# A two-layer encoder on one core: the low part of every second weight group of the first FFN by a negation and an accumulating DMA

## The chip, the cores and the metric

One core of a Trainium2 chip runs the whole kernel. The metric is the device time of one execution in microseconds (us). The kernel before takes 2468.03 us, the median of two runs.

## What is computed

A trunk of two layers over 256 tokens of width 2048, in float32. Layer 0 has differential attention beside a gated MLP over chunks, layer 1 a gated linear recurrence in both directions. After each mixer stands a SwiGLU feed-forward block (FFN) with 5632 hidden features, and the change lies in the first of the two:

```
def swiglu(h, w_gate, w_up, w_down):
    return (jax.nn.silu(h @ w_gate) * (h @ w_up)) @ w_down

    hn = rms_norm(h, ffn_norm[l])
    h = h + swiglu(hn, ffn_w_gate[l], ffn_w_up[l], ffn_w_down[l])
```

## The kernel before

All weight products go through one function, `stream` (L101). It multiplies the 256 tokens (two blocks of 128, each with its own PSUM bank) with 512 columns of a weight matrix, over a list of weight groups. A group is 512 rows by 512 columns, 1 MB, laid out in HBM as one contiguous piece and in SBUF as 128 partitions x 4 x 512.

The products keep float32 precision by splitting. Activations x and weights w are each the sum of a high part, rounded to the type float32r, and a low part, the rest. Per group:

- SP loads the group into `raw` (L114), a tile of a pool with three buffers.
- ACT copies it to `whi` (L121), which rounds it. Three buffers.
- DVE subtracts `whi` from `raw` into `wlo` (L122). Two buffers.
- PE does 24 matmuls, for each of 4 row blocks and 2 token blocks three: x high by w high (L136), x high by w low (L137), x low by w high (L138).

The copy and the subtraction are issued with a priority that places them up to 400 instructions ahead on their engines (`AHEAD`), so ACT and DVE prepare groups ahead of PE as far as the buffers go. A copy has to wait until PE has done with the group three before it, a load until `raw` of the group three before it has been read by ACT and DVE.

`ffn` (L232) runs in two passes over the hidden blocks, 6 and then 5 of them, 512 features each. For each block it calls `stream` for gate and for up, with 4 groups each. After a pass it calls `stream` four times for down, with 6 and then 5 groups each. In between stand a sigmoid on ACT (L249), products on DVE (L250, L255), and transposes of the result by PE with copies by ACT (L173) and subtractions by DVE (L174). The first FFN has 22 x 4 + 4 x 6 + 4 x 5 = 132 groups. Its hidden blocks are held in a pool `hp` (L234). GpSimd (POOL) has nothing but one small power (L153) to do in that stage.

Of the kernel before, what the change touches and what calls it, by code (L numbers as in the profile page):

```python
# [11 lines left out]
F32 = mybir.dt.float32  # L12
# [8 lines left out]
P = 128  # L21
# [3 lines left out]
KG = 4  # L25
# [12 lines left out]
def _ap(base, offset, dims):  # L38
    """View of a tile: its partitions, then [stride, count] dims from `offset`."""
    return bass.AP(base.tensor, base.offset + offset, [list(base.ap[0])] + [list(d) for d in dims])  # L40
# [6 lines left out]
class Lazy:  # L47
    """Operands that are emitted one by one, in order, when they are asked for."""

# [11 lines left out]
def trunk(ctx: ExitStack, tc: tile.TileContext, ins, out):  # L61
# [22 lines left out]

    # ---- work that is emitted in pieces between the groups of a stream
    pieces = []
# [12 lines left out]

    # ---- shared pieces  # L100
    def stream(w, nb, kgs, xs, name, after=None, fine=False, by_block=False):  # L101
        """Two PSUM banks (token blocks) of x @ w[:, nb], over the K groups `kgs`, xs.get(i) the operand of kgs[i]."""
        ps = [ps_mm.tile([P, NB], F32, tag="mm", name=f"{name}_ps{b}") for b in range(2)]
        last = len(kgs) - 1
        held = []
        xs.get(0)
        for i, kg in enumerate(kgs):
            raw = wpool.tile([P, KG, NB], F32, tag="raw", name=f"{name}_raw{i}")
            whi = wpool.tile([P, KG, NB], F32R, tag="whi", name=f"{name}_whi{i}")
            wlo = wpool.tile([P, KG, NB], F32R, tag="wlo", name=f"{name}_wlo{i}", bufs=WLO_BUFS)  # L110
            step = 1 if fine and i == 0 else KG
            for k in range(0, KG, step):
                d = slice(k, k + step)
                nc.sync.dma_start(raw[:, d], w[nb, kg, :, d])  # L114
                with ExitStack() as order:
                    if not fine:
                        order.enter_context(tc.high_priority(offset=AHEAD))
                    elif i == 0 and k > 0:
                        order.enter_context(tc.issue_after(marks["act"]))
                        order.enter_context(tc.issue_after(marks["dve"]))  # L120
                    nc.scalar.copy(whi[:, d], raw[:, d])  # L121
                    nc.vector.tensor_tensor(wlo[:, d], raw[:, d], whi[:, d].bitcast(F32), op=ALU.subtract)  # L122
            if i < last:
                xs.get(i + 1)
            held.append((i, xs.get(i), whi, wlo))
            if by_block and i == last - 1:
                continue
            order = [(g, k, b) for g in held for k in range(KG) for b in range(2)]
            if by_block and i == last:
                order = [(g, k, b) for b in range(2) for g in held for k in range(KG)]  # L130
            held = []
            for n, ((j, (xh, xl), hi, lo), k, b) in enumerate(order):
                sl = slice(b * P, (b + 1) * P)
                first = j == 0 and k == 0
                end = j == last and k == KG - 1
                nc.tensor.matmul(ps[b], xh[:, k, sl], hi[:, k, :], start=first, stop=False)  # L136
                nc.tensor.matmul(ps[b], xh[:, k, sl], lo[:, k, :], start=False, stop=False)  # L137
                nc.tensor.matmul(ps[b], xl[:, k, sl], hi[:, k, :], start=False, stop=end)  # L138
                if n == KG - 1:
                    tick()  # L140
            if after is not None:
                after(i)
            tick()
        return ps
# [16 lines left out]
    def to_T(src, pool, tag, name, gains=None):  # L161
        """Token-major [P, 2, 512] to feature-major high and low parts [P, 4, 256]."""
        xh = pool.tile([P, KG, S], F32R, tag=tag, name=f"{name}_hi")
        xl = pool.tile([P, KG, S], F32R, tag=tag, name=f"{name}_lo")
        for half in range(2):
            tp = ps_tr.tile([P, 2, S], F32, tag="tr", name=f"{name}_tp{half}")
            for c in range(2):
                f0 = (half * 2 + c) * P
                for b in range(2):
                    nc.tensor.transpose(tp[:, c, b * P:(b + 1) * P], src[:, b, f0:f0 + P], ident)  # L170
            if gains is None:
                d = slice(half * 2, half * 2 + 2)
                nc.scalar.copy(xh[:, d, :], tp)  # L173
                nc.vector.tensor_tensor(xl[:, d, :], tp, xh[:, d, :].bitcast(F32), op=ALU.subtract)  # L174
            else:
                for c in range(2):
                    k = half * 2 + c
                    g = gains[k]
                    marks["act"] = nc.scalar.activation(xh[:, k, :], tp[:, c, :], AF.Copy, scale=g).ins
                    marks["dve"] = nc.vector.scalar_tensor_tensor(  # L180
                        out=xl[:, k, :], in0=tp[:, c, :], scalar=g, in1=xh[:, k, :].bitcast(F32),
                        op0=ALU.mult, op1=ALU.subtract).ins
        return xh, xl
# [4 lines left out]
    def mean_square(tiles, name):  # L188
        """Calls that add a tile's part each; the last one leaves the rsqrt in the list."""
        ss = small.tile([P, 2, 4], F32, tag="ss", name=f"{name}_ss")  # L190
# [41 lines left out]
    def ffn(l, xs, rstd, following):  # L232
        """SwiGLU in two passes over the hidden blocks; `following` takes the last pass's hooks."""
        with tc.tile_pool(name=f"hT{l}", bufs=12, reuse_waits="tile") as hp:  # L234
            for blocks in (range(0, 6), range(6, 11)):
# [6 lines left out]
                for j in blocks:  # L242
                    n = f"f{l}_{j}"
                    pg = stream(ins["w_gate"][l], j, ALLK, xs, f"{n}g", after=late)
                    gs = []
                    for b in range(2):
# [4 lines left out]
                        gs.append(sg)  # L251
                    pu = stream(ins["w_up"][l], j, ALLK, xs, f"{n}u")
                    hh = tmp.tile([P, 2, NB], F32, tag="hh", name=f"{n}_hh", bufs=2)
# [5 lines left out]
                for nb in range(4):  # L259
                    pd = stream(ins["w_down"][l], nb, list(blocks), hts, f"f{l}d{blocks[0]}_{nb}",  # L260
                                after=(lambda i, nb=nb: following(nb, i)) if last else None,
                                by_block=last and l == 1 and nb == 3)
                    if last and l == 1:
# [3 lines left out]

    # ---- layer 0 mixer
    xs, rstd, squares = norm(SM_MIX, "e", load=True)
# [29 lines left out]
    def gelu(nb, name, **kw):  # L299
        """gelu(y) as 0.5 y (1 + tanh(c (y + 0.044715 y^3))), with yh = y / 2."""  # L300
        ps, t = proj(nb, name, **kw)
# [11 lines left out]
    def attention(half, qt, kt, vt, o):  # L313
        """Four heads; one head's scores run while another's softmax is at work."""
        qks, es, aTs = {}, {}, {}
# [166 lines left out]

    # ---- layer 1 mixer
    odd = ExitStack()
# [13 lines left out]
    def scan_pair(pair, qt, ft, vt, o):  # L498
        """Two heads. A[t, s] = sum_k q_t k_s prod(decays between), built for ever larger blocks: in each
        block of 2m positions the queries of one half and the keys of the other meet at the boundary."""  # L500
        n = f"s{pair}"
# [16 lines left out]
        for d in range(2):  # L518
            tp = transposed(ft[1 - d], f"tf{d}")
            for i in range(2):  # L520
                hd = pair * 2 + i
                nc.vector.tensor_scalar(F[:, d, i, :], tp[:, i, :], omlb[:, 1 - d, hd:hd + 1], lb[:, 1 - d, hd:hd + 1],
                                        op0=ALU.mult, op1=ALU.add)
            # F holds the backward decays first, K the forward keys first
            nc.vector.tensor_scalar(K[:, 1 - d], F[:, d], -1.0, 1.0, op0=ALU.mult, op1=ALU.add)
# [15 lines left out]
        diag = _ap(A, 0, [[512, 2], [384, 2], [1, P]])  # L541
        # each position with itself, then level by level the pairs that meet there
        sc = scores("ld", lambda i, b: kd[:, i, b * P:(b + 1) * P], lambda i, b: qs[:, i, b * P:(b + 1) * P])
# [48 lines left out]
    for hg in range(4):  # L592
# [4 lines left out]
        if hg == 0:  # L597
# [3 lines left out]
            nc.gpsimd.tensor_copy(masks, mraw[:, 0:7])  # L601
            # softmax over the two layers, then the second one's cumulative sum less the first
            lraw = sm[:, SM_LB:SM_LB + 64].rearrange("p (d l h) -> p d l h", d=2, l=2)
# [57 lines left out]

    # ---- last FFN and the final norm
    fp = ctx.enter_context(tc.tile_pool(name="fin", bufs=1, reuse_waits="tile"))
# [36 lines left out]
def _blocks(w):  # L700
    """[K, N] as [N / 512, K / 512, 128, 4, 512], so that one load is one contiguous piece."""
    k, n = w.shape
# [3 lines left out]
def _cols(a):  # L706
    """[..., n * 128] as [128, ... * n]: features on partitions."""
    a = np.asarray(a)
# [15 lines left out]
def _masks():  # L724
    """[s, which, t]: for each m the pairs in one block of 2m but not in one half of it."""
    i = np.arange(P)
# [48 lines left out]
```

## Time and profile before

| | before |
|---|---|
| median of two runs | 2468.03 us (2466.86 to 2469.21) |
| span of the profiled execution | 2467.0 us |
| busy: PE, DVE, ACT, POOL | 99%, 56%, 42%, 3% |
| share of the 16 DMA engines' time | 52% |
| HBM read | 441.61 MB |

The profile gives no time of the profiled execution apart from its span; that span lies within the range of the two runs and 1.0 us below their median. Names in the rows leave out numbers, so `f_2g` stands for the gate stream of hidden block 2 in both FFNs, while `f0d` is the down stream of the first FFN alone. An "idle before" with an arrow names what ended the wait.

### The profile page before, as it was taken

The numbers are of one execution on the slowest core, as the hardware profiler recorded it, in microseconds if no ns is written. First come the engines' busy times: TensorE is split into PE (matmuls) and PEld (weight loads), VectorE is DVE, ScalarE is ACT, GpSimd is POOL, SyncE is SP. The second block draws the span as 40 slices with busy tenths as digits, with TensorE's granted clock in tenths as the row PEclk, the third lists the DMA queues.
The fourth block names the chain that finished last, engine by engine and source line by source line (L and its number), as shares of the span: only waits on it lengthen the run. The fifth ranks groups of instructions, "written<-read, shape, count | busy, mean of one in ns | idle before, by whom it ended". The sixth has DMA issues, their size and how long they took to land.

```text
span 2467.0 us, 27323 instructions
## 1 busy us (share of the span) xinstructions
PE 2446.4 (99%) x11392; PEld 2033.3 (82%) x11392; DVE 1373.6 (56%) x1192; ACT 1030.8 (42%) x952; POOL 72.3 (3%) x71
## 2 busy tenths in 40 slices
PE   8999999999999999999999999999999999999998
PEld 7887888888888888888888888888888888888887
DVE  5668655454444554444768585855545454444544
ACT  5445444333333343444444444454443433334433
POOL 0003000000000000000000000000000000000001
PEclk9999999999999999999999999999999999999999
DMA  7444455555555555555444444455555555555553
GB/s 270 168 163 162 157 186 188 190 194 188 186 190 192 188 188 188 188 191 191 154 154 154 154 140 156 148 178 192 188 188 192 188 188 188 193 193 188 193 188 136
DMA packets 63132, 445.48 MB, mean 181 GB/s; under 512 B 6944, under 2 KB 7200, under 8 KB 9760
## 3 DMA queue, kind: packets, MB, share of 16 engines
q1 hardware_dynamic: 62576, 442.13, 52.1%
q8 instruction: 89, 1.46, 0.2%
q10 hardware_dynamic: 432, 1.60, 0.2%
q14 instruction: 35, 0.29, 0.0%
HBM read 441.61 MB, written 2.10 MB: 180 GB/s over the span
## 4 chain that ended last, share of the span: by engine, by line
PE 97%; DVE 2%; POOL 1%; issue 0%; DMA 0%; ACT 0%; POOLq 0%; ACTq 0%; DVEq 0%
PE f0d_ps L137 3%; PE f0d_ps L138 3%; PE f0d_ps L136 3%; PE f1d_ps L137 3%; PE f1d_ps L136 3%; PE f1d_ps L138 3%; PE c_f_ps L136 2%; PE c_f_ps L138 2%; PE c_f_ps L137 2%; PE s_l L535 2%; PE c_q_ps L137 1%; PE c_q_ps L136 1%; PE c_q_ps L138 1%; PE cout_ps L138 1%; PE eout_ps L138 1%; PE cout_ps L136 1%
## 5 line engine op out<-in xcount | busy, mean ns | idle before, releaser
L122 DVE TENSOR_TENSOR f0d_wlo<-f0d_raw,f0d_whi 128x2048 fp32r<-128x2048 f32 x44 | 100.8, 2290 | 108.2 <-PE f0d_ps L137 80.9
L122 DVE TENSOR_TENSOR f1d_wlo<-f1d_raw,f1d_whi 128x2048 fp32r<-128x2048 f32 x44 | 100.8, 2290 | 106.1 <-PE f1d_ps L137 82.4
L121 ACT CAST f0d_whi<-f0d_raw 128x2048 fp32r<-128x2048 f32 x44 | 84.3, 1917 | 153.4 <-PE f0d_ps L138 111.5
L121 ACT CAST f1d_whi<-f1d_raw 128x2048 fp32r<-128x2048 f32 x44 | 84.3, 1916 | 151.9 <-PE f1d_ps L138 103.5
L122 DVE TENSOR_TENSOR c_f_wlo<-c_f_raw,c_f_whi 128x2048 fp32r<-128x2048 f32 x32 | 73.3, 2292 | 71.8 <-PE c_f_ps L137 60.4
L136 PE MATMUL c_f_ps<-c_f_whi,c_hi 128*128 128x512 f32 x256 | 101.9, 398 | 0.0
L137 PE MATMUL c_f_ps<-c_f_wlo,c_hi 128*128 128x512 f32 x256 | 99.7, 390 | 0.0
L138 PE MATMUL c_f_ps<-c_f_whi,c_lo 128*128 128x512 f32 x256 | 99.7, 389 | 0.0
L121 ACT CAST c_f_whi<-c_f_raw 128x2048 fp32r<-128x2048 f32 x32 | 61.2, 1914 | 76.7 <-PE c_f_ps L138 56.9
L535 PEld LDWEIGHTS s_l<-s_Q,s_kc 128*128 128x128 f32 x448 | 61.5, 191 | 4.4
L555 ACT COPY s_kc<-s_K 128x512 f32<-128x512 f32 x56 | 37.2, 664 | 65.0 <-PE s_l L535 35.4
L535 PE MATMUL s_l<-s_Q,s_kc 128*128 128x128 f32 x448 | 62.8, 284 | 0.0
L138 PEld LDWEIGHTS c_f_ps<-c_f_whi,c_lo 128*128 128x128 f32 x256 | 48.0, 188 | 10.0
L137 PEld LDWEIGHTS c_f_ps<-c_f_wlo,c_hi 128*128 128x128 f32 x256 | 48.2, 188 | 9.1
L136 PEld LDWEIGHTS c_f_ps<-c_f_whi,c_hi 128*128 128x128 f32 x256 | 48.2, 188 | 9.0
L122 DVE TENSOR_TENSOR c_i_wlo<-c_i_raw,c_i_whi 128x2048 fp32r<-128x2048 f32 x16 | 40.2, 2512 | 25.1 <-PE c_f_ps L137 18.9
L122 DVE TENSOR_TENSOR cout_wlo<-cout_raw,cout_whi 128x2048 fp32r<-128x2048 f32 x16 | 36.6, 2290 | 31.3 <-PE cout_ps L137 21.0
L136 PE MATMUL c_g_ps<-c_g_whi,c_hi 128*128 128x512 f32 x128 | 52.2, 408 | 0.0
L122 DVE TENSOR_TENSOR eout_wlo<-eout_raw,eout_whi 128x2048 fp32r<-128x2048 f32 x16 | 36.6, 2289 | 28.0 <-PE eout_ps L137 16.7
L136 PE MATMUL c_q_ps<-c_q_whi,c_hi 128*128 128x512 f32 x128 | 52.1, 407 | 0.0
L136 PE MATMUL c_i_ps<-c_i_whi,c_hi 128*128 128x512 f32 x128 | 51.7, 404 | 0.0
L559 DVE TENSOR_TENSOR s_Q<-s_Q,s_F 128x512 f32<-128x512 f32 x56 | 42.1, 752 | 17.1 <-PE s_l L535 16.9
(691 smaller groups left out, 7307.1 us busy)
## 6 DMA issues: line engine op xcount, KB each, us to landing
f0d_raw<-in_w_down SPq DMA_DIRECT2D x44, 1024.0 KB, 4.9
f1d_raw<-in_w_down SPq DMA_DIRECT2D x44, 1024.0 KB, 4.8
c_f_raw<-in_hgrn_w_in SPq DMA_DIRECT2D x32, 1024.0 KB, 4.8
eout_raw<-in_even_w_out SPq DMA_DIRECT2D x16, 1024.0 KB, 4.9
c_i_raw<-in_hgrn_w_in SPq DMA_DIRECT2D x16, 1024.0 KB, 4.9
c_q_raw<-in_hgrn_w_in SPq DMA_DIRECT2D x16, 1024.0 KB, 4.9
c_g_raw<-in_hgrn_w_in SPq DMA_DIRECT2D x16, 1024.0 KB, 4.9
cout_raw<-in_hgrn_w_out SPq DMA_DIRECT2D x16, 1024.0 KB, 4.9
```

Of the source, the lines that this page charges most:

```text
L121: nc.scalar.copy(whi[:, d], raw[:, d])
L122: nc.vector.tensor_tensor(wlo[:, d], raw[:, d], whi[:, d].bitcast(F32), op=ALU.subtract)
L136: nc.tensor.matmul(ps[b], xh[:, k, sl], hi[:, k, :], start=first, stop=False)
L137: nc.tensor.matmul(ps[b], xh[:, k, sl], lo[:, k, :], start=False, stop=False)
L138: nc.tensor.matmul(ps[b], xl[:, k, sl], hi[:, k, :], start=False, stop=end)
L535: nc.tensor.matmul(sc[:, i, b, :], stat(i, b), mov(i, b), start=True, stop=True)
L555: nc.scalar.copy(kc, _ap(K, 0, dims))
L559: nc.vector.tensor_tensor(_ap(X, 0, dims), _ap(X, 0, dims), by, op=ALU.mult)
```

## The change

`stream` gets a new argument, `summed`: a pool, given by `ffn` in its three calls for layer 0 (its own pool `hp`), and not given for layer 1 or anywhere else. Where it is given, groups with an odd number in their stream get their low part in another way. ACT writes the negative of `whi` into a new tile `slo` of that pool (two buffers). Then POOL issues a DMA that reads the same group of raw weights from HBM a second time and adds it to what stands in `slo`. DVE does nothing for these groups. The tile `raw` is still loaded for them, since ACT copies it to `whi`. Even groups are treated as before. Apart from comments that are left out, this is all of it; line numbers after `stream` move by 8.

```
     def stream(w, nb, kgs, xs, name, after=None, fine=False, by_block=False, summed=None):
...
-            wlo = wpool.tile([P, KG, NB], F32R, tag="wlo", name=f"{name}_wlo{i}", bufs=WLO_BUFS)
+            by_dma = summed is not None and i % 2 == 1
+            if by_dma:
+                wlo = summed.tile([P, KG, NB], F32R, tag="slo", name=f"{name}_slo{i}", bufs=2)
+            else:
+                wlo = wpool.tile([P, KG, NB], F32R, tag="wlo", name=f"{name}_wlo{i}", bufs=WLO_BUFS)
...
                     nc.scalar.copy(whi[:, d], raw[:, d])
-                    nc.vector.tensor_tensor(wlo[:, d], raw[:, d], whi[:, d].bitcast(F32), op=ALU.subtract)
+                    if by_dma:
+                        nc.scalar.mul(wlo[:, d], whi[:, d].bitcast(F32), -1.0)
+                        nc.gpsimd.dma_start(wlo[:, d], w[nb, kg, :, d], accum_op=ALU.add)
+                    else:
+                        nc.vector.tensor_tensor(wlo[:, d], raw[:, d], whi[:, d].bitcast(F32), op=ALU.subtract)
...
-                    pg = stream(ins["w_gate"][l], j, ALLK, xs, f"{n}g", after=late)
+                    pg = stream(ins["w_gate"][l], j, ALLK, xs, f"{n}g", after=late, summed=hp if l == 0 else None)
...
-                    pu = stream(ins["w_up"][l], j, ALLK, xs, f"{n}u")
+                    pu = stream(ins["w_up"][l], j, ALLK, xs, f"{n}u", summed=hp if l == 0 else None)
...
-                                by_block=last and l == 1 and nb == 3)
+                                by_block=last and l == 1 and nb == 3, summed=hp if l == 0 else None)
```

The first place is ACT's queue at the step from the gate to the up stream of hidden block 2 (`f0_2g`, `f0_2u`; `sg` is the sigmoid, `1T` the transposed hidden block 1). Before:

```order
L121 CAST f0_2g_whi2_3413<-f0_2g_raw2_3412 128x2048
L121 CAST f0_2g_whi3_3443<-f0_2g_raw3_3442 128x2048
L121 CAST f0_2u_whi0_3481<-f0_2u_raw0_3480 128x2048
L173 CAST f0_1T_hi_3396<-f0_1T_tp0_3398 128x512
L173 CAST f0_1T_hi_3396<-f0_1T_tp1_3405 128x512
L121 CAST f0_2u_whi1_3511<-f0_2u_raw1_3510 128x2048
L249 ACTIVATE f0_2_sg0_3472<-f0_2g_ps0_3334,f0_rstd_2878 128x512
L121 CAST f0_2u_whi2_3541<-f0_2u_raw2_3540 128x2048
L249 ACTIVATE f0_2_sg1_3475<-f0_2g_ps1_3335,f0_rstd_2878 128x512
L121 CAST f0_2u_whi3_3571<-f0_2u_raw3_3570 128x2048
```

And after the change, at the same place:

```order
L125 CAST f0_2g_whi2_3422<-f0_2g_raw2_3421 128x2048
L125 CAST f0_2g_whi3_3452<-f0_2g_raw3_3451 128x2048
L127 ACTIVATE f0_2g_slo3_3453<-f0_2g_whi3_3452 128x2048
L125 CAST f0_2u_whi0_3491<-f0_2u_raw0_3490 128x2048
L181 CAST f0_1T_hi_3405<-f0_1T_tp0_3407 128x512
L181 CAST f0_1T_hi_3405<-f0_1T_tp1_3414 128x512
L125 CAST f0_2u_whi1_3521<-f0_2u_raw1_3520 128x2048
L127 ACTIVATE f0_2u_slo1_3522<-f0_2u_whi1_3521 128x2048
L257 ACTIVATE f0_2_sg0_3482<-f0_2g_ps0_3342,f0_rstd_2879 128x512
L125 CAST f0_2u_whi2_3552<-f0_2u_raw2_3551 128x2048
L257 ACTIVATE f0_2_sg1_3485<-f0_2g_ps1_3343,f0_rstd_2879 128x512
L125 CAST f0_2u_whi3_3582<-f0_2u_raw3_3581 128x2048
```

The copies keep their order, and each odd one is followed at once by its negation (L127).

The second place is PE, at the first matmuls of group 1 of the up stream of hidden block 2, with the semaphores that each waits for (`DVE`, `Activation`: those engines; `DMASW`: a DMA issued by POOL). Before:

```order
L138 MATMUL f0_2u_ps1_3479<-f0_2u_whi0_3481,f00_lo_2616 128x512
L136 MATMUL f0_2u_ps0_3478<-f0_2u_whi1_3511,f01_hi_2669 128x512 [waits Activation_49]
L137 MATMUL f0_2u_ps0_3478<-f0_2u_wlo1_3512,f01_hi_2669 128x512 [waits DVE_49]
L138 MATMUL f0_2u_ps0_3478<-f0_2u_whi1_3511,f01_lo_2670 128x512
L136 MATMUL f0_2u_ps1_3479<-f0_2u_whi1_3511,f01_hi_2669 128x512
```

And after the change:

```order
L146 MATMUL f0_2u_ps1_3489<-f0_2u_whi0_3491,f00_lo_2616 128x512
L144 MATMUL f0_2u_ps0_3488<-f0_2u_whi1_3521,f01_hi_2669 128x512 [waits Activation_49]
L145 MATMUL f0_2u_ps0_3488<-f0_2u_slo1_3522,f01_hi_2669 128x512 [waits DMASW2_49]
L146 MATMUL f0_2u_ps0_3488<-f0_2u_whi1_3521,f01_lo_2670 128x512
L144 MATMUL f0_2u_ps1_3489<-f0_2u_whi1_3521,f01_hi_2669 128x512
```

PE's order is the same; the second matmul of an odd group waits for the DMA into `slo` in place of DVE.

The third place is POOL's queue around the same groups, with the waits of each. Before, POOL has `f0_rstd` as its only instruction between the gMLP and the end of the first FFN; after the change it issues 64 DMAs there, of which these are five:

```order
L128 DMA f0_1u_slo3_3310<-in_w_up0 128x2048 [waits DMASW5_49,PE_49,Activation_49]
L128 DMA f0_2g_slo1_3376<-in_w_gate0 128x2048 [waits DMASW6_49,PE_49,Activation_49]
L128 DMA f0_2g_slo3_3453<-in_w_gate0 128x2048 [waits DMASW7_49,PE_49,Activation_49]
L128 DMA f0_2u_slo1_3522<-in_w_up0 128x2048 [waits DMASW0_49,PE_49,Activation_49]
L128 DMA f0_2u_slo3_3583<-in_w_up0 128x2048 [waits DMASW1_49,PE_49,Activation_49]
```

Each waits for its negation (`Activation`), for PE having read the tile's earlier content, and for an earlier DMA of this kind; nothing else stands between them.

## Rows read from the trace of the kernel before

**Rows 1.** The page's parts 1 and 4: busy time by engine; chain that ended last.

```profile
PE 2446.4 (99%) x11392; PEld 2033.3 (82%) x11392; DVE 1373.6 (56%) x1192; ACT 1030.8 (42%) x952; POOL 72.3 (3%) x71
...
PE 97%; DVE 2%; POOL 1%; issue 0%; DMA 0%; ACT 0%; POOLq 0%; ACTq 0%; DVEq 0%
```

**Rows 2.** All waits of PE: who waited for whom, total us, times, longest.

```profile
PE e_tp L170 <- DMA h<-in_x: 5.5, 1, 5.5
PE s_tf L514 <- DVE s_F L522: 3.1, 4, 0.8
PE sv L446 <- POOL e_b0t L438: 2.5, 1, 2.5
PE e_tp L170 <- DVE e_q_wlo L122: 1.3, 1, 1.3
```

**Rows 3.** The window of the first FFN: busy us by engine, clock, DMA share.

```profile
core 0: us, PE busy (x) PEld busy (x) DVE busy (x) ACT busy (x) POOL busy (x), PEclk, DMA share, GB/s
361.00:1093.00 732.00, 732.00 (x3266) 603.39 (x3265) 360.13 (x232) 288.81 (x208) 0.71 (x1) 1.00 0.55 188
```

**Rows 4.** Timeline of ACT, 458 to 492 us: start, duration, instruction, idle before.

```profile
460.95 1.92 ACT L121 CAST f_2u_whi<-f_2u_raw 128x2048 fp32r<-128x2048 f32 x1 [3.53 <-PE f_2g_ps L138]
462.76 1.07 ACT L173 CAST f_1T_hi<-f_1T_tp 128x512 fp32r<-128x512 f32 x2
467.28 1.92 ACT L121 CAST f_2u_whi<-f_2u_raw 128x2048 fp32r<-128x2048 f32 x1 [3.45 <-PE f_2g_ps L138]
472.04 0.69 ACT L249 ACTIVATE f_sg<-f_2g_ps,f_rstd 128x512 f32<-128x512 f32 x1 [2.84 <-PE f_2g_ps L138]
472.72 1.92 ACT L121 CAST f_2u_whi<-f_2u_raw 128x2048 fp32r<-128x2048 f32 x1
474.54 0.67 ACT L249 ACTIVATE f_sg<-f_2g_ps,f_rstd 128x512 f32<-128x512 f32 x1
478.20 1.92 ACT L121 CAST f_2u_whi<-f_2u_raw 128x2048 fp32r<-128x2048 f32 x1 [2.99 <-issue]
483.60 1.92 ACT L121 CAST f_3g_whi<-f_3g_raw 128x2048 fp32r<-128x2048 f32 x1 [3.48 <-PE f_2u_ps L138]
489.08 1.93 ACT L121 CAST f_3g_whi<-f_3g_raw 128x2048 fp32r<-128x2048 f32 x1 [3.57 <-PE f_2u_ps L138]
```

**Rows 5.** Timeline of PE where the gate stream of block 2 ends.

```profile
472.29 0.39 PE L138 MATMUL f_2g_ps<-f_2g_whi,f_lo 128*128 128x512 f32 x1
...
472.52 0.39 PE L136 MATMUL f_2u_ps<-f_2u_whi,f_hi 128*128 128x512 f32 x1
```

**Rows 6.** Down stream: groups of instructions (busy us, mean ns), and SP's waits for DVE.

```profile
L122 DVE TENSOR_TENSOR f0d_wlo<-f0d_raw,f0d_whi 128x2048 fp32r<-128x2048 f32 x44 | 100.8, 2290 | 108.2 <-PE f0d_ps L137 80.9
...
L121 ACT CAST f0d_whi<-f0d_raw 128x2048 fp32r<-128x2048 f32 x44 | 84.3, 1917 | 153.4 <-PE f0d_ps L138 111.5
...
SPq L114 <- DVE f0d_wlo L122: 230.5, 44, 6.1
```

**Rows 7.** Loads of the up stream of block 2 (issue, landing), and of f0d (landing).

```profile
L114 SPq DMA_DIRECT2D f_2u_raw<-in_w_up x8: 327/328/328, 452.4 to 1836.0; - x8
...
DMA to landing us min/median/max: 4.7/4.8/6.1
...
DMA to landing us min/median/max: 4.7/4.9/6.9
```

**Rows 8.** POOL: its longest wait, and two of its short instructions (busy us, mean ns).

```profile
POOL c_rstd L153 <- DVE c_ms L158: 736.8, 1, 736.8
...
L153 POOL TENSOR_TENSOR e_rstd<-e_ms,mhalf 128x2 f32<-128x2 f32 x1 | 0.7, 716 | 33.0 <-DVE e_ms L158 33.0
...
L293 POOL TENSOR_TENSOR e_q0r<-e_q0t,sm 128x128 f32<-128x128 f32 x1 | 0.4, 440 | 0.0
```

**Rows 9.** Around PE's wait for POOL: windows (clock last but two), timeline of PE.

```profile
240.00:246.00 6.00, 3.46 (x11) 2.51 (x10) 5.93 (x6) 2.08 (x4) 5.21 (x3) 0.76 0.81 300
246.00:250.00 4.00, 4.00 (x22) 3.41 (x21) 2.82 (x4) 1.66 (x2) 0.00 (x0) 0.93 0.00 0
...
243.59 2.08 PE L446 MATMUL sv<-e_b0t,wsT 128*128 128x256 f32 x4 [2.54 <-POOL e_b0t L438]
245.10 0.99 PE L136 MATMUL e_u_ps<-e_u_whi,e_hi 128*128 128x512 f32 x1
245.89 0.63 PE L137 MATMUL e_u_ps<-e_u_wlo,e_hi 128*128 128x512 f32 x1
```

More of the change, by code (lines that the diff above doesn't have):

```diff
@@ L98, in finish_pieces, with stream @@
             tick()
-    def stream(w, nb, kgs, xs, name, after=None, fine=False, by_block=False):
+    def stream(w, nb, kgs, xs, name, after=None, fine=False, by_block=False, summed=None):
         ps = [ps_mm.tile([P, NB], F32, tag="mm", name=f"{name}_ps{b}") for b in range(2)]
```

## The prediction

> **What bounds the kernel now.** I read the busy shares and the chain of work that ended last first. TensorE (PE) is busy for 99% of the span, DVE 56%, ACT 42% [rows 1], and the chain is 97% PE. A matmul's modelled end says little, so the second view is who kept PE waiting. Over 2467.0 us there are four such waits, 12.4 us in all, none in the first FFN: their lines are the transposes of x, the scan and the gMLP product [rows 2]. The windows then cut out the first FFN, 361 to 1093 us: PE is busy in all of it, the granted clock is 1.00, DVE works 360 us, ACT 289 us, POOL 0.7 us, and the 16 DMA engines are 55% busy [rows 3]. So the subtraction that the change removes keeps nobody waiting there. At best the time stays.
>
> The stage holds 132 weight groups: 22 streams of four for gate and up, four down streams of six, four of five. One group takes PE 5.45 us: ACT's copies begin at 472.72, 478.20, 483.60 and 489.08 [rows 4]. I call this g, so 2g = 10.9 us.
>
> What sets the order is the three whi buffers. The copy for group i waits for the last matmul of group i-3 (the releaser of nearly all ACT waits is a PE line 138, [rows 4, 6]). It starts 0.2 us after that group's end: PE opens the next stream at 472.52 and ACT's copy starts at 472.72 [rows 4, 5]. PE needs the low part of group i with that group's second matmul, 0.2 us into it. From the release of the buffer to that need lie two groups: 10.9 + 0.2 = 11.1 us. Before the change the chain in this interval is copy 1.92, then subtraction 2.29 [rows 6], about 4.4 us of work.
>
> **The change, part by part.** An odd group is taken off DVE in each stream: 44 in gate and up, 4 x 3 + 4 x 2 = 20 in down, 64 in all.
>
> *Removed:* 64 subtractions, 64 x 2.29 = 147 us of DVE [rows 6]. Worth 0 us: DVE has 372 us idle in the stage and PE never waits for it [rows 2, 3].
>
> *Added on ACT:* 64 negations of 128x2048. The nearest row is the copy of the same shape, 1.92 us [rows 6]: 123 us more, 289 to 412 of 732. The order rows show each behind its own copy and ahead of the next copy. Two copies, one negation and the largest company (two sigmoids, two transposed copies, 2.4 us, [rows 4]) make 8.2 us in 10.9, so ACT doesn't become the bound. Each negation fits into the 3.5 us in which ACT now waits for PE [rows 4]. Without that cover each would cost 1.92 us, 123 us in all.
>
> *Loads by SP:* the buffer of an odd group's raw weights comes free after the copy, no longer after the subtraction. SP now waits for DVE [rows 6], so these loads start some 2 us earlier or more. Worth 0; it gives the loads slack for the next point.
>
> *Added DMA:* 64 transfers of 1 MB that read the weights a second time, add them to what stands in SBUF, and write it back. No row shows such a transfer. POOL is free for the issue: it waits through the stage [rows 8]. An odd group's low part now comes by hand-over 0.2, copy 1.92, a hand-over of 0.1, negation 1.92, then X, the time from there to the landing. L = 4.1 + X. It is hidden if L is at most 11.1, so X at most 7.0.
>
> If it is later, PE waits W at the second matmul of odd group i. In the interval that counts lies group i-2, which is odd too and may have waited itself. So W(i) + W(i-2) = L - 11.1: the waits can be equal or alternate between the full L - 11.1 and nothing. The first late one finds no wait before it, so I expect them to alternate: 32 waits of L - 11.1. While PE waits, copies, subtractions and loads wait with it; nothing else is late next.
>
> X, from both sides. *Low:* a load of 1 MB from SP takes 4.8 us from issue to landing and 0.33 us to issue [rows 7], X = 5.1, all hidden. *What a load takes of the DMA engines:* 55% of 5.55 us a group (732 / 132) = 3.05 us per MB [rows 3]; the other 1.8 of the 4.8 us are fixed. *High:* three passes over the megabyte (two reads, one write, none overlapping) are 9.15 us, and a whole load of another group in between: X = 1.8 + 9.15 + 3.05 + 0.3 = 14.3. *Taken:* two passes, since a load already reads and writes one megabyte in its 3.05 us and only one read is added: 6.1 us. Half a load shares the engines with it (1.5 us; the loads are busy for half the time), and POOL takes 0.5 us to issue (its short instructions take 0.44 to 0.72 us, [rows 8]). X = 1.8 + 6.1 + 1.5 + 0.5 = 9.9.
>
> The Trainium skill bears on this doubling ("Collectives: The Full Stack", Part 3, the bandwidth ceiling). It says that a DMA reduction is slower than a copy by its second source read, not by the add, and about half as fast. By it the transfer would again be 6.1 us; no row here shows it.
>
> So L = 14.0 and L - 11.1 = 2.9 us, 32 times: 93 us. The average period of two groups is then 10.9 + 1.45 = 12.35 us. The DMA engines need 2 x 3.05 + 6.1 = 12.2 of it: nearly full, but not yet the bound.
>
> *The clock.* The trace has one PE wait of this size. It waited 2.54 us before the gMLP product at 243.59; the granted clock is 0.76 over 240 to 246 and 0.93 over 246 to 250, and matmuls after it show 0.99 and 0.63 us, where the usual is 0.39 [rows 5] [rows 9]. With the lower level half of the upper (1.2 of 2.4 GHz) that is 2 x 0.24 x 6 + 2 x 0.07 x 4 = 3.4 us at the low level, 1.7 us lost. If each of 32 waits brings this, 54 us.
>
> Sum: 2467.0 + 93 + 54 = 2614 us of profiled span. The runs' median, 2468.0, lies 1.0 above that span: 2615 us. Differences under 2% (49 us) can't be told from no change here.
>
> **The rivals.**
>
> *Hidden, about the same.* If the two reads overlap, or the engines take an accumulating transfer hardly longer than a load, X is 5.1 to 7 and PE never waits: 2468 us. For it: 45% of DMA time is free, and the loads have slack. Against it: the bytes read double, and the window X has is only 2.2 us more than a load's 4.8. It stays within 2% up to W = 0.77 us a transfer on average (1.5 us by turns, which may be too short for the clock), that is X up to 11.1 + 1.54 - 4.1 = 8.5 us. This rival ends on the other side, and X = 8.5 decides.
>
> A rule of the Trainium skill supports it ("DMA: Bandwidth & Descriptors", Anatomy of one DMA, SWDGE path): 2.0 us plus bytes over 436 GB/s, an estimate of 4.4 us for 1 MB from GpSimd. It is for plain copies; by it X is under 7 and the time 2468 us.
>
> *DMA becomes the bound.* If the transfer takes three passes, the engines need 6.1 + 9.15 = 15.25 us per pair of groups against PE's 10.9: 64 x 4.35 = 278 us, 2746 us. PE then waits at every odd group, and its clock no longer matters. At four passes it is 18.3 us and 2942 us. For it: nothing in the trace bounds the cost of the read-modify-write. Against it: the longest landing of the 44 down loads is 6.9 us against a median of 4.9 [rows 7], so queueing alone doesn't multiply a transfer.
>
> *Faster.* It would need PE to gain. It has no wait in the stage, and the matmuls stay the same, so only a chance effect.
>
> **How the numbers follow.** Waits by the chain (about 2520 to 2680): 0.45, and the point is its time. Hidden or nearly: 0.25. DMA-bound or dearer: 0.28. Faster: 0.02. So faster 0.02, same 0.25, slower 0.73. The likeliest case's own range is 2530 to 2650 (X 9 us without the clock's part: 32 x 2.0 = 64 us; X 11 us with it: 32 x 3.9 + 54 = 179 us). The range for 8 in 10 takes in the hidden case and the three passes: 2464 to 2770, leaving out 0.02 below and some 0.15 above.
>
> **What would show it.** In the profile after: L145 matmuls that wait for a DMA into slo, some 32 of 3 us by turns; landing of these transfers near 9.4 us after issue; ACT up by 123 us and DVE down by 147; DMA busy share in the stage 0.95 or more; granted clock below 1.00 there. Landings under 7 us and no PE wait show the hidden case. A DMA share of 1.0 with waits at every odd group, and loads that land late too, show the DMA bound. The prediction is wrong if POOL takes microseconds to issue a transfer, or if the doubled read costs much more or less than 3 us.

## The result and the profile after

The kernel after takes 2531.97 us (median of two runs, 2529.54 to 2534.41), before 2468.03: the ratio is 1.026, 95% interval 1.023 to 1.029. The change makes the kernel 64 us slower. The direction was forecast and 2532 lies in the range, but the size is off: the forecast was 2615, 147 us slower. The profiled execution has a span of 2527.8 us, 60.8 more than before.

The page of after, parts 1, 3 and 4 (busy time; DMA queues with packets, MB and share of the 16 engines; chain that ended last):

```profile
PE 2465.0 (98%) x11392; PEld 2030.5 (80%) x11392; DVE 1228.9 (49%) x1128; ACT 1150.8 (46%) x1016; POOL 127.7 (5%) x135
...
q1 hardware_dynamic: 62576, 442.13, 50.2%
q0 software_dynamic: 9216, 67.11, 13.7%
...
PE 81%; DMA 14%; DVE 2%; issue 2%; POOL 1%; ACT 0%; SPq 0%; POOLq 0%; ACTq 0%; DVEq 0%
```

Against [rows 1], PE's share falls from 99% to 98%, and the chain now holds 14% DMA where it had none. The 64 new transfers are queue q0. They move 67 MB, and their packets take 13.7% of the engines' time, 0.137 x 2527.8 / 64 = 5.4 us for each megabyte.

The windows that cut out the first FFN, first of before (up to 1096, so that both hold the same 3278 matmuls), columns as in [rows 3]:

```profile
361.00:1096.00 735.00, 735.00 (x3278) 605.83 (x3277) 362.37 (x232) 290.71 (x209) 0.71 (x1) 1.00 0.55 188
```

And of after, the same work as a whole, then four stretches of it:

```profile
361.00:1157.00 796.00, 753.77 (x3278) 604.42 (x3277) 217.09 (x166) 408.52 (x272) 55.09 (x64) 0.99 0.93 258
366.00:378.00 12.00, 8.30 (x28) 6.65 (x29) 0.00 (x0) 3.46 (x3) 0.91 (x1) 0.72 1.00 297
378.00:690.00 312.00, 298.75 (x1307) 239.11 (x1306) 87.00 (x68) 166.03 (x108) 22.38 (x26) 1.00 0.93 260
697.00:705.00 8.00, 7.10 (x24) 5.70 (x25) 0.00 (x0) 1.30 (x1) 0.86 (x1) 0.79 0.94 268
705.00:1157.00 452.00, 430.41 (x1883) 346.12 (x1882) 125.26 (x94) 231.71 (x155) 30.23 (x35) 1.00 0.92 257
```

The stage is 61 us longer, the whole loss. DVE works 145 us less, ACT 118 us more, the DMA share goes from 0.55 to 0.93. The clock, 1.00 over the whole stage before, falls in two short stretches only.

The waits of PE in after (who waited for whom: us in total, times, longest), which answer to [rows 2]:

```profile
PE f0d_ps L145 <- DMA f0d_slo<-in_w_down: 13.0, 10, 3.2
...
PE f_0g_ps L145 <- DMA f_0g_slo<-in_w_gate: 4.2, 1, 4.2
...
PE f_0u_ps L145 <- DMA f_0u_slo<-in_w_up: 2.9, 2, 1.9
...
PE f_9u_ps L145 <- DMA f_9u_slo<-in_w_up: 2.4, 1, 2.4
...
PE f_2u_ps L145 <- DMA f_2u_slo<-in_w_up: 1.7, 2, 1.3
```

The second matmul of an odd group (L145) waits for the DMA into `slo`, as in the forecast, but briefly. All such waits together are 42 us by this view. Counted by the starts of the 64 matmuls (how much later than the usual 0.23 us each begins after the one before it), they are 49 us, on average 0.77 us each. From 829 to 935 us they are 0, 1.1, 0.2, 0, 1.1, 0, 1.2, 0, 0.9, 0: by turns, as W(i) + W(i-2) = L - 11.1 asks. Elsewhere they are less regular, since single landings run from 7.7 to 11.6 us: two neighbours add up to 0.2 to 4.3 us, 1.5 us on average. Taken with each transfer's own landing the formula still fits (correlation 0.81 over the 63 pairs).

One transfer in the timelines of ACT, POOL and PE of after (start, duration, instruction, idle before):

```profile
481.51 1.91 ACT L125 CAST f_2u_whi<-f_2u_raw 128x2048 fp32r<-128x2048 f32 x1 [3.48 <-PE f_2g_ps L146]
483.45 1.92 ACT L127 ACTIVATE f_2u_slo<-f_2u_whi 128x2048 fp32r<-128x2048 f32 x1
...
485.66 0.86 POOL L128 DMA_DIRECT2D f_2u_slo<-in_w_up  x1 [11.88 <-ACT f_2u_slo L127]
...
493.44 0.50 PE L145 MATMUL f_2u_ps<-f_2u_slo,f_hi 128*128 128x512 f32 x1 [0.41 <-DMA f_2u_slo<-in_w_up]
```

Copy and negation take 1.9 us each, as in [rows 4] and the forecast. The negation ends at 485.37, POOL begins to issue 0.29 us later, and this takes it 0.86 us. How long a transfer then takes from the start of its issue is a line of the tile `f0d_slo` in after (20 transfers):

```profile
DMA to landing us min/median/max: 7.8/8.1/10.7
```

The median of all 64 is 8.1 us too. So X = 0.3 + 8.1 = 8.4 us, where 9.9 was taken. The loads of `f0d_raw` land after 5.0 us, where [rows 7] has 4.9.

### The profile page after: what moved, and what is told of

It reads as the page before. It is cut to its first block, busy times and chain, and to the rows that moved or that the text cites. A ratio compares the mean times of both kernels' runs of the same rounds, so it can differ in the third digit from the quotient of the medians.

```text
span 2527.8 us, 27362 instructions
## 1 busy us (share of the span) xinstructions
PE 2465.0 (98%) x11392; PEld 2030.5 (80%) x11392; DVE 1228.9 (49%) x1128; ACT 1150.8 (46%) x1016; POOL 127.7 (5%) x135
## 3 DMA queue, kind: packets, MB, share of 16 engines
q0 software_dynamic: 9216, 67.11, 13.7%
## 4 chain that ended last, share of the span: by engine, by line
PE 81%; DMA 14%; DVE 2%; issue 2%; POOL 1%; ACT 0%; SPq 0%; POOLq 0%; ACTq 0%; DVEq 0%
DMA f0d_slo<-in_w_down 3%; PE f1d_ps L144 3%; PE f1d_ps L146 3%; PE f1d_ps L145 3%; PE c_f_ps L144 2%; PE c_f_ps L145 2%; PE c_f_ps L146 2%; PE s_l L543 2%; PE f0d_ps L145 2%; PE f0d_ps L146 2%; PE f0d_ps L144 2%; PE c_q_ps L145 1%; PE cout_ps L146 1%; PE c_q_ps L144 1%; PE cout_ps L144 1%
## 5 line engine op out<-in xcount | busy, mean ns | idle before, releaser
L130 DVE TENSOR_TENSOR f1d_wlo<-f1d_raw,f1d_whi 128x2048 fp32r<-128x2048 f32 x44 | 100.8, 2291 | 106.0 <-PE f1d_ps L145 82.4
L130 DVE TENSOR_TENSOR f0d_wlo<-f0d_raw,f0d_whi 128x2048 fp32r<-128x2048 f32 x24 | 55.0, 2293 | 146.0 <-ACT f0d_whi L125 146.0
L130 DVE TENSOR_TENSOR c_f_wlo<-c_f_raw,c_f_whi 128x2048 fp32r<-128x2048 f32 x32 | 73.3, 2292 | 71.8 <-PE c_f_ps L145 60.4
L145 PE MATMUL c_f_ps<-c_f_wlo,c_hi 128*128 128x512 f32 x256 | 99.7, 390 | 0.0
L145 PEld LDWEIGHTS c_f_ps<-c_f_wlo,c_hi 128*128 128x128 f32 x256 | 48.2, 188 | 9.0
L130 DVE TENSOR_TENSOR c_i_wlo<-c_i_raw,c_i_whi 128x2048 fp32r<-128x2048 f32 x16 | 40.2, 2512 | 26.4 <-PE c_f_ps L145 18.9
L125 ACT CAST eout_whi<-eout_raw 128x2048 fp32r<-128x2048 f32 x16 | 30.7, 1917 | 48.0 <-PE eout_ps L146 29.6
L130 DVE TENSOR_TENSOR cout_wlo<-cout_raw,cout_whi 128x2048 fp32r<-128x2048 f32 x16 | 36.7, 2291 | 31.1 <-PE cout_ps L145 21.1
L125 ACT CAST cout_whi<-cout_raw 128x2048 fp32r<-128x2048 f32 x16 | 30.7, 1918 | 44.1 <-PE cout_ps L146 31.3
```

## The experiments

All stand beside the kernel before on the same chip. The diffs are against the kernel after. Matmul line numbers differ by one to three between the kernels.

**The new work without the dependency (e_unread).** DVE subtracts for all groups as before; the negations and the accumulating transfers run too, into a tile that nobody reads.

```
-                wlo = summed.tile([P, KG, NB], F32R, tag="slo", name=f"{name}_slo{i}", bufs=2)
-            else:
-                wlo = wpool.tile([P, KG, NB], F32R, tag="wlo", name=f"{name}_wlo{i}", bufs=WLO_BUFS)
+                slo = summed.tile([P, KG, NB], F32R, tag="slo", name=f"{name}_slo{i}", bufs=2)
+            wlo = wpool.tile([P, KG, NB], F32R, tag="wlo", name=f"{name}_wlo{i}", bufs=WLO_BUFS)
...
                     nc.scalar.copy(whi[:, d], raw[:, d])
+                    nc.vector.tensor_tensor(wlo[:, d], raw[:, d], whi[:, d].bitcast(F32), op=ALU.subtract)
                     if by_dma:
-                        nc.scalar.mul(wlo[:, d], whi[:, d].bitcast(F32), -1.0)
-                        nc.gpsimd.dma_start(wlo[:, d], w[nb, kg, :, d], accum_op=ALU.add)
-                    else:
-                        nc.vector.tensor_tensor(wlo[:, d], raw[:, d], whi[:, d].bitcast(F32), op=ALU.subtract)
+                        nc.scalar.mul(slo[:, d], whi[:, d].bitcast(F32), -1.0)
+                        nc.gpsimd.dma_start(slo[:, d], w[nb, kg, :, d], accum_op=ALU.add)
```

> The kernel before (DVE subtracts for every group) with the 64 negations and the 64 accumulating DMAs added into a tile that nothing reads. PE waits for none of it. Chain: 2468 to 2475 us, with a DMA share in the stage near 1.0. DMA engines: loads land late and PE or ACT waits for them, 2500 or more. Interference: matmul steps in the stage above 230 ns on average, 2480 to 2490.

Measured: 2468.58 us, ratio 1.0001 (0.9992 to 1.0011). Its window of the stage:

```profile
361.00:1093.00 732.00, 732.00 (x3266) 603.39 (x3265) 360.76 (x232) 408.22 (x272) 55.10 (x64) 1.00 0.97 280
```

And the landings of `f0d_slo` in it:

```profile
DMA to landing us min/median/max: 8.5/10.9/13.6
```

With the DMA engines 97% busy and transfers that land after 10.9 us, PE loses nothing. The load on the engines is no loss by itself, nor are matmuls slower for it (3266 in 732 us, as before); the loss needs the matmul that waits. That rules out the DMA bound as the cause. The same with the DMA's line left out as well, so 64 negations that nobody reads (e_neg_only):

> The kernel before with the 64 negations added (into a tile that nothing reads), and no DMA from POOL. Chain and DMA engines: 2468, within 3 us of before, ACT busy 289 + 123 = 412 us in the stage. If ACT's extra work itself costs, up to 64 x 1.92 = 123 us more.

Measured: 2468.37 us, ratio 1.0001 (0.9992 to 1.0011). ACT's added work is hidden.

**A longer chain (e_neg_twice).** A second pass of ACT over `slo` before the transfer, 1.92 us more in L:

```
                         nc.scalar.mul(wlo[:, d], whi[:, d].bitcast(F32), -1.0)
+                        nc.scalar.mul(wlo[:, d], whi[:, d].bitcast(F32), 1.0)
```

> The changed kernel with a second ACT pass over slo (whi times 1, then whi times -1): 1.92 us more ahead of each DMA. Chain with waits that alternate (W(i) + W(i-2) = L - 11.1): 32 x 1.92 = 61 us more than the changed kernel, 2593, and up to 50 more where waits over 3 us make the clock fall: 2593 to 2645. If every transfer paid by itself: 64 x 1.92 = 123 more, 2655. DMA engines: no more than the changed kernel, 2532 to 2540.

Measured: 2628.46 us, ratio 1.0651 (1.0630 to 1.0672). The window of the stage, and PE's longest waits:

```profile
361.00:1253.00 892.00, 790.66 (x3271) 635.27 (x3270) 216.39 (x167) 523.94 (x336) 55.12 (x64) 0.94 0.82 230
```

```profile
PE f0d_ps L146 <- DMA f0d_slo<-in_w_down: 31.0, 10, 4.2
...
PE f_5u_ps L146 <- DMA f_5u_slo<-in_w_up: 3.5, 1, 3.5
```

The late starts sum to 107 us, 58 more than in after; 32 x 1.92 = 61 by the alternation, where a wait at each of the 64 would have added 123. They are 3.3 us on average and 0 by turns. And now the clock comes in: 892 - 732 - 107 = 53 us of the stage are no wait, at a granted clock of 0.94. By the starts, 206 matmuls follow in steps of 0.43 us, the lower level, in place of 0.23: 41 us. The second matmul after each wait, which also starts late, makes 8 us more. In after this rest is 796 - 735 - 49 = 12 us.

**Half the bytes (e_half); no addition (e_plain).** In the first kernel DVE subtracts row blocks 0 and 1 of an odd group, and the transfer does 2 and 3, 512 KB:

```
-                        nc.scalar.mul(wlo[:, d], whi[:, d].bitcast(F32), -1.0)
-                        nc.gpsimd.dma_start(wlo[:, d], w[nb, kg, :, d], accum_op=ALU.add)
+                        nc.vector.tensor_tensor(wlo[:, 0:2], raw[:, 0:2], whi[:, 0:2].bitcast(F32), op=ALU.subtract)
+                        nc.scalar.mul(wlo[:, 2:4], whi[:, 2:4].bitcast(F32), -1.0)
+                        nc.gpsimd.dma_start(wlo[:, 2:4], w[nb, kg, :, 2:4], accum_op=ALU.add)
```

> Half the size: in odd groups DVE subtracts the first two of the four row blocks and the negation and the accumulating DMA (512 KB) do the other two. Chain: negation 1.0 us, landing about 8.1 - 2.7 = 5.4 us after issue, needed 2.7 us later than before: L = 0.2 + 1.92 + 1.0 + 0.3 + 5.4 = 8.8 against 13.8: 2468 to 2472 us. A fixed price for each transfer, whatever its size, would leave it above 2500.

Measured: 2469.91 us, ratio 1.0008 (0.9997 to 1.0018), and no PE wait for a transfer in the stage. But the landing is not the 5.4 us expected:

```profile
DMA to landing us min/median/max: 7.6/8.4/9.4
```

Here DVE reads `raw` too and frees it later, so that a load is issued within 0.3 us of 62 of the 64 transfers. The packets of half the bytes do take less (3.6 us, the table below), but 4.5 us pass between the issue and the first one. So this run doesn't show what half the bytes save in landing. PE doesn't wait since it reads blocks 2 and 3 only with the 14th matmul of the group (the first two blocks take 12), some 2.7 us later. In the second kernel the transfer overwrites `slo` instead of adding, so the low part there is the whole weight:

```
-                        nc.gpsimd.dma_start(wlo[:, d], w[nb, kg, :, d], accum_op=ALU.add)
+                        nc.gpsimd.dma_start(wlo[:, d], w[nb, kg, :, d])
```

> The changed kernel with POOL's DMA writing the raw weights into slo instead of adding them (this leaves out the addition: the low part of odd groups is wrong). One read and one write of 1 MB in place of two reads and one write, all waits and the order the same. Chain: landing about 8.1 - 2.4 = 5.7 us after issue, L = 4.1 + 0.3 + 5.7 = 10.1, under 11.1: 2468 to 2475 us, DMA share of the stage about 0.8. If the second read is not what makes the transfer late (POOL's issue, or the queue of POOL itself), landing stays near 8 us and the time near 2530.

Measured: 2471.39 us, ratio 1.0014 (1.0004 to 1.0025). Its transfers in the page's part 3, and their landings:

```profile
q0 software_dynamic: 9216, 67.11, 7.1%
```

```profile
DMA to landing us min/median/max: 5.1/5.4/7.2
```

The same bytes in the same queue take 0.071 x 2469.6 / 64 = 2.74 us of the engines without the addition, 5.4 with it: the factor is 2.0, and 2.7 us of landing go with it. Without these 2.7 us little is lost: PE waits three times for a transfer, 0.7 us in all, and the time is 4 us above that of before. The Trainium skill ("Collectives: The Full Stack", Part 3, the bandwidth ceiling) says that a reduction by DMA runs at about half a copy's rate, because it reads two sources. The factor of 2.0 agrees; the reason isn't shown, as e_plain leaves out the second source and the addition together. The Trainium skill's fit for a transfer from GpSimd ("DMA: Bandwidth & Descriptors", Anatomy of one DMA), an estimate of 4.4 us for 1 MB, is 1 us below the 5.4 measured for the plain one.

**Two transfers of 512 KB in place of one (e_split),** so that PE could start on the first half:

```
-                        nc.gpsimd.dma_start(wlo[:, d], w[nb, kg, :, d], accum_op=ALU.add)
+                        for c in (slice(0, 2), slice(2, 4)):
+                            nc.gpsimd.dma_start(wlo[:, c], w[nb, kg, :, c], accum_op=ALU.add)
```

> The changed kernel with each accumulating DMA split into two of 512 KB, for the first and the last two row blocks; same bytes, same chain, but PE's first need (11.1 us) hangs on the first half alone, its second (13.8 us) on the last. Chain: first half 4.1 + 0.3 + 5.4 = 9.8, last half 4.1 + 0.3 + 0.9 + 8.1 = 13.4: both in time, 2468 to 2480. DMA engines as the bound, or a price per transfer: 2530 or more.

Measured: 2508.34 us, ratio 1.0163 (1.0143 to 1.0184). Some is won, not all, against an expected 2468 to 2480; PE's largest wait:

```profile
PE f0d_ps L146 <- DMA f0d_slo<-in_w_down: 6.9, 13, 1.2
```

Taken by themselves, the 64 first halves land 7.6 us after their issue (median), not the 5.4 expected. With that L = 4.1 + 0.3 + 7.6 = 12.0, still past 11.1. Why half the bytes take 7.6 us here was not tested; the stage's DMA share is 0.97.

**An earlier start.** The negation reads `raw` instead of `whi`, so it need not wait for the copy, which waits for PE. First without an order of its own (e_neg_first):

```
-                    nc.scalar.copy(whi[:, d], raw[:, d])
                     if by_dma:
-                        nc.scalar.mul(wlo[:, d], whi[:, d].bitcast(F32), -1.0)
+                        nc.scalar.mul(wlo[:, d], raw[:, d], -1.0)
                         nc.gpsimd.dma_start(wlo[:, d], w[nb, kg, :, d], accum_op=ALU.add)
+                        nc.scalar.copy(whi[:, d], raw[:, d])
                     else:
+                        nc.scalar.copy(whi[:, d], raw[:, d])
```

> Odd groups: ACT negates straight from the raw weights, before the copy to whi, so the negation no longer waits for the whi buffer that PE releases, only for the raw load and for slo; it and the DMA can start up to one group (5.45 us) earlier. The work and the bytes are those of the changed kernel. Theory of the chain (the time is 32 x (L - 11.1), L the time from the buffer's release to the landing): L falls by 1.92 us at least, from 12.5 to 10.6 or less, so PE never waits: 2468 to 2475 us. Theory of the DMA engines (busy 0.93 of the stage, so loads and accumulating transfers get in each other's way): little gained, 2515 us or more. Theory of interference (more ACT and DMA work makes each matmul slower): waits go, but 2480 to 2490.

Measured: 2520.52 us, ratio 1.0209 (1.0194 to 1.0225), far from the expected 2468. ACT's timeline shows one reason:

```profile
450.28 1.92 ACT L126 ACTIVATE f_2g_slo<-f_2g_raw 128x2048 fp32r<-128x2048 f32 x1 [6.62 <-DMA f_2g_raw<-in_w_gate]
452.10 1.89 ACT L130 CAST f_2g_whi<-f_2g_raw 128x2048 fp32r<-128x2048 f32 x1
```

The scheduler put the odd group's negation ahead of the even group's copy (L130). It waits 6.6 us for its load, the copy waits behind it, and PE then waits for DVE's low part of even groups too. So a second kernel (e_neg_ordered) holds the negation behind the copy of the group before:

```
+                        with tc.issue_after(marks["whi"]):
+                            nc.scalar.mul(wlo[:, d], raw[:, d], -1.0)
...
                     else:
+                        marks["whi"] = nc.scalar.copy(whi[:, d], raw[:, d]).ins
```

> As e_neg_first (odd groups negated straight from the raw weights), but ACT's order is held: the negation of odd group i stands behind the copy of group i-1 and ahead of its own copy, so no copy of an even group stands behind a negation of the next group. It waits for its raw load and slo, not for the whi buffer. Theory of the chain: the DMA can be issued 4 us after the end of group i-4 if the load has landed, needed 16.5 us after it, L is far below the time there is: no PE wait, 2468 to 2475 us. If e_neg_first's 2520 us came from DMA engines or from the negation's place ahead of the release rather than from its order on ACT, this stays at 2510 or more.

Measured: 2521.95 us, ratio 1.0224 (1.0207 to 1.0241). This missed as well. The order was as wanted, but the transfers of `f0d_slo` (first line) and the loads of `f0d_raw` (second line) both land late:

```profile
DMA to landing us min/median/max: 11.1/12.5/13.4
...
DMA to landing us min/median/max: 5.8/10.2/12.6
```

Its timelines of POOL and SP show how they meet:

```profile
445.97 0.86 POOL L128 DMA_DIRECT2D f_2g_slo<-in_w_gate  x1 [9.94 <-ACT f_2g_slo L127]
...
446.21 0.33 SPq L118 DMA_DIRECT2D f_2g_raw<-in_w_gate  x1
```

A transfer and a load are issued within 0.24 us (within 0.3 us at 38 of the 64 transfers), and by the medians of `f0d_slo` a transfer lands 4.4 us later than in after. What is gained at the start is lost at the landing, in the load that the next group needs too.

**Fewer transfers.** Only group 1 of each stream goes by DMA, 30 of them instead of 64 (e_one):

```
-            by_dma = summed is not None and i % 2 == 1
+            by_dma = summed is not None and i == 1
```

> The changed kernel with group 1 of each stream alone by negation and DMA: 30 transfers, not 64; the others by DVE. Chain with waits that share (W(i) + W(i-2) = L - 11.1): here group i-2 is never late, so each transfer is late by the whole L - 11.1 = 12.6 - 11.1 = 1.5 us, 30 x 1.5 = 45 us and 30 x 0.1 us for PE's restart: 2512 to 2520, four fifths of the changed kernel's loss with less than half of its transfers. A price for each transfer by itself: 30/64 of 64 us, 2498. DMA engines as the bound (their share falls from 0.93 to about 0.75): 2468 to 2475.

Measured: 2705.79 us, ratio 1.0970 (1.0952 to 1.0989). Less than half the transfers cost almost four times as much, against an expected 2512 to 2520. PE's waits, the window of the stage, the landings:

```profile
PE f0d_ps L145 <- DMA f0d_slo<-in_w_down: 39.6, 8, 5.6
```

```profile
361.00:1330.00 969.00, 809.45 (x3258) 650.89 (x3258) 294.44 (x200) 341.08 (x236) 25.73 (x30) 0.90 0.55 174
```

```profile
DMA to landing us min/median/max: 11.6/12.1/12.6
```

The formula holds: X = 0.3 + 12.1, L = 16.5, and since group i-2 isn't late here, each of the 30 waits the full L - 11.1 = 5.4 us, 162 us; the late starts sum to 164. The rest of the stage's growth, 969 - 732 - 164 = 73 us, goes with the clock of 0.90: 306 matmuls in steps of 0.43 us make 61 us of it. What I had not foreseen is the landing. The engines are only 55% busy, but each of the 30 transfers is issued less than 3 us behind two loads, where after has one: in the timelines SP issues loads from 505.15 and 505.57, POOL its transfer at 507.37. The same 30 transfers with the earlier, ordered negation (both edits above, e_one_ordered):

> As e_neg_ordered (negation from the raw weights, ahead of its own copy and behind the copy of the group before) but for group 1 of each stream alone, 30 transfers. e_neg_ordered's remaining 54 us are put down to contention: there the transfer and the loads started together, landing rose from 8.1 to 12.5 us for the transfer and from 5.0 to 10.2 for the loads. With 30 transfers the engines are busy for about 0.75, so the landings should be near 9 and 6 us, and the chain, begun earlier, is in time: 2468 to 2475 us. If the rest came from the order of ACT's work and not from the DMA engines, half of it stays: 2490 to 2500.

Measured: 2469.11 us, ratio 1.0006 (0.9996 to 1.0015), no PE wait for a transfer, landings of 9.0 us. With room on the engines (a share of 0.73 in the stage), no load in the 3 us before 22 of the 30 transfers, and the earlier start, the transfer is hidden.

**What a landing is made of.** I counted the packets of the trace for each whole transfer: the time from its first packet's start to its last packet's end, and how much of the loads moved in that time. Medians over the transfers of `f0d_slo`, in us and MB; "the rest" is the landing less the packets' time:

| kernel (label) | landing | first to last packet | the rest | loads in it |
|---|---|---|---|---|
| after | 8.1 | 6.1 | 2.1 | 0.19 |
| e_neg_twice | 8.1 | 6.2 | 1.9 | 0.12 |
| e_one_ordered | 9.0 | 6.8 | 2.4 | 0.49 |
| e_unread | 10.9 | 7.9 | 2.4 | 1.01 |
| e_neg_ordered | 12.5 | 8.4 | 4.3 | 1.21 |
| e_one | 12.1 | 7.4 | 4.8 | 0.86 |
| e_half (512 KB) | 8.4 | 3.6 | 4.8 | 0.17 |
| e_plain (no addition) | 5.4 | 3.4 | 2.1 | 0.11 |

Within e_unread, e_neg_ordered and e_one a straight line through those transfers that had no other beside them gives 4.9 to 5.0 us plus 2.7 to 3.1 us per MB of loads, about what a load takes of the engines (3.05). Where two loads were issued in the 3 us before (e_one) or one at the same time (e_half, most of e_neg_ordered), 2 to 3 us more pass ahead of the first packet. In after one load is issued 2.2 us ahead of each transfer, when the odd group's copy frees `raw`, and the next 6.4 us behind it (medians), so that the transfer's packets run nearly alone. PE's waits aren't what sets this phase: e_plain, where PE hardly waits, has 2.2 and 5.6 us. That the phase is what holds X at 8.4 is read from these counts; no run moved the loads alone.

No version here is faster than before: in the kernel before, PE is never idle in that stage, so there is nothing to gain by taking work off DVE.

## Why the prediction was right in direction and wrong in size

- *PE is the bound, DVE's 147 us are worth nothing:* held. e_neg_only and e_unread show that ACT's added work and the traffic cost nothing either. Forecast for the stage: ACT 412, DVE 213; measured 409 and 217.
- *The deadline of 11.1 us, and W(i) + W(i-2) = L - 11.1 by turns:* held. e_neg_twice (58 us more for 61) and e_one (164 us for 162) follow it; after does on average (49 us for 45), but strictly by turns only in part of the stage.
- *X = 9.9 us:* this step failed; X is 8.4. Two of its terms were too large. The two passes, 6.1 us, are 5.4. Half a load sharing, 1.5 us, is 0.19 MB x 3 = 0.6. The fixed parts came out right, 1.8 + 0.5 taken, 2.1 + 0.3 measured, though the 0.5 was misread: a landing already counts from the start of the issue (so does the 4.8 of the lower bound), and the 0.3 that is measured is the hand-over to POOL, which had no term. The sum of the measured ones is 5.4 + 0.6 + 2.4 = 8.4. A small error, but L - 11.1 is a difference: 1.4 us instead of 2.9, so 32 x 1.4 = 45 us (49 measured) instead of 93.
- *The clock, 32 x 1.7 = 54 us:* failed with it, and was the larger miss in proportion. In after the clock falls only behind the two waits of 4.2 and 3.2 us. With half of full speed as the lower level, these are 2 x 0.28 x 12 = 6.7 and 2 x 0.21 x 8 = 3.4 us at it, 5 us lost. The mean of one case, a wait of 2.5 us [rows 9], was applied to waits that came out half as long. e_neg_twice, with waits of 3.3 us, pays about what the term had forecast for waits of 2.9, 53 us, of which 41 us go with matmuls at the lower level.
- *What makes up the 61 us:* 49 of waits, 5 of clock. After a wait the first matmul is recorded with 0.50 us where 0.39 is usual, and the next starts 0.11 us later; over the 41 late ones that is 5 us, and 2 are left.
- *The range of the likeliest case:* for X = 11 it should add 32 x 4.0, not 32 x 3.9, 3 us more; nothing hangs on it.
- *Rival "hidden":* it fell, narrowly. It put the border at X = 8.5 and 0.77 us a transfer on average; both came out on it, 8.4 and 0.77, and the clock and the restarts carried the result past 2%. Its condition was right: e_plain (5.4 us) is hidden.
- *Rival "DMA bound":* it fell. One transfer costs two passes, not three, and e_unread moves all of them in 732 us with PE busy throughout. The forecast share of 0.95 or more is 0.93.

## What to carry to other kernels

To price a step that is put on another path, find the buffer release that starts its chain and the instruction that needs it: the loss is the excess over that interval, and a small error in the chain (14.0 us for 12.5) can be half of the excess (2.9 for 1.4). The accumulating DMA here took the DMA engines twice as long as the same transfer without the addition (5.4 us against 2.74), and its landing was its own time plus that of the loads that happened to run ahead of it and beside it; starting it earlier helped where it didn't start together with a load (e_one_ordered) and not where it did (e_neg_ordered), though these two differ in the number of transfers as well. Where TensorE is busy throughout, as in this stage, relieving another engine earns nothing (e_one_ordered: DVE 65 us less in the stage, the time the same), and each microsecond put between a buffer and its matmul can cost.

## What the runs showed of the hardware that was not expected

- The landing of the same 1 MB accumulating transfer has a median of 8.1, 9.0, 10.9, 12.1 or 12.5 us, by when loads are issued around it, and the busy share doesn't tell which: 12.1 at a share of 0.55 (e_one), 8.1 at 0.93 (after).
- Less than half the transfers, in another phase, cost almost four times as much (e_one, +238 us against +64).
- POOL takes 0.86 us to issue an accumulating transfer of 1 MB or of 512 KB, and 0.53 us for a plain one of 1 MB.
- The length of PE's wait alone doesn't decide whether the granted clock falls to the lower level. Taken by the starts of the matmuls, it fell in after at the waits of 4.3 and 3.4 us and at none of the other 24 of 0.9 to 2.5 us; in e_neg_twice at 28 of 32 (2.4 to 4.3 us; the four others had 3.0 to 3.2 us); in e_neg_ordered at one of 3.0 and one of 2.4 us (0.83 over 588 to 598 us and over 898 to 908) but not at one of 3.2. In [rows 9] a single wait of 2.54 us, with other work around it, lowered it as well.
